# Laying out a convolution stage anew: more weight pairs in one product, low parts and tap sums on GpSimd, one-chunk first blocks, norm sums in two parts

## The chip, the core and the metric

The kernel runs on one core of a Trainium2 chip. The time is device microseconds of one execution, the median of several runs. A profile comes from one execution of its own, whose time is given beside it. In the rows, PE is TensorE's matmul side and PEld its weight load, DVE is VectorE, ACT is ScalarE, POOL is GpSimd (called Pool here) and SP is SyncE, whose queue issues the transfers. L226 is line 226 of the kernel's file.

## The reference

Two decoder layers are computed for a prompt of 256 positions and a group of 8 samples of one position each; the kernel treats them as T = 264 columns. The width is D = 2048, 16 chunks of 128 channels. Only the first mixer of the first layer is touched:

```python
def conformer_conv(x, past, w_in, b_in, w_dw, b_dw, ln_g, ln_b, w_out, b_out):
    a, gt = jnp.split(x @ w_in + b_in, 2, axis=-1)
    u = a * jax.nn.sigmoid(gt)
    y, new_past = causal_dwconv(u, past, w_dw, b_dw)      # 31 taps along the positions, per channel
    y = jax.nn.silu(layer_norm(y, ln_g, ln_b))
    return y @ w_out + b_out, new_past
```

Behind it come a ConvFFN, the per-layer embedding, an mLSTM mixer and a second ConvFFN, all with large weight products.

## The kernel before

Features lie on partitions, positions along the free axis. A weight product goes through `wblock`: it loads raw FP32 weights in buffers of four 128-row chunks (pool `rawp`, three buffers), and takes the chunks in pairs. A pair is normally split: ScalarE casts its high part (`whi`, L234), VectorE or Pool subtracts it from the raw weights to get the low part (`wlo`, L235), and TensorE forms three products per tile, `XH` by `whi`, `XL` by `whi` and `XH` by `wlo` (L250, L252, L253; L259 is the same product with `XL`, issued later). Where the argument `native` says so, the pair stays whole: one FP32 product of the raw weights with `X` (L226), which the trace records as two instructions. High and low parts have five buffers each (pool `hlp`), accumulators in PSUM six (`psA`), and U two (`psM`).

`conv_mixer` runs over `BLOCKS`, each of one or two chunks. A block forms for each chunk a gate and a value with `wblock` over all 16 input chunks (8 pairs). Then, per chunk:

- ScalarE takes the sigmoid of the gate (L546), VectorE writes U, the gated value, to PSUM (a `stt`), ScalarE copies it to SBUF (L555) and starts the sum: tap 30 with the bias into `Y` (L557), tap 29 into `Z`, a piece of `cscr` (L559).
- Taps 28 downward are shared out. The first `GT` of them: ScalarE scales (L564) into a ring in `cscr`, Pool adds into `Z`. The next `PT`: TensorE multiplies by diagonal matrices (L588), which Pool prepares at the start (L504), at the end of the stage (`late`). The rest: VectorE, one `stt` a tap from U into `Y`.
- `join` adds `Z` to `Y` on VectorE.

`SCM` says at which blocks the sample state is multiplied by its taps and reduced (four chunks at a time, on VectorE). `PLO` gives the number of low parts in 8 that Pool takes in each block, `NAT` the number of pairs left whole. In the last block `ln_pre` forms the layer norm's shift (a mean of chunks 0 to 11), subtracts it from those chunks and sums their squares; `ln` adds chunks 12 to 15, normalizes, and its results go into the first block of `cv_w_out`.

The order of each engine's instructions is made by a scheduler when the program is built, within the data's dependences; `high_priority` moves some ahead. Each engine then works through its queue in that order, so an instruction that waits holds everything behind it.

## Time and profile before

| | us |
|---|---|
| median of 3 runs (2585.0 to 2591.87) | 2591.32 |
| the profiled execution | 2594.45 |
| its span, first to last instruction | 2592.6 |
| TensorE busy, matmul | 2524.0 |
| VectorE busy | 1680.9 |
| ScalarE busy | 1286.0 |
| Pool busy | 395.2 |

The convolution stage fills the first tenth of the span: its weight products run from 4.3 us, and the first product with `cv_w_out` starts at 266.06 us. Over half of Pool's busy time lies in it. Records of matmuls overlap, so a busy TensorE is not one at its peak; the number of matmuls in a stretch tells more. Records of VectorE in a run overlap a little as well. A `stt` is shown as SCALAR_TENSOR_TENSOR at L141, an addition or subtraction by `tt` as TENSOR_TENSOR at L138, whichever engine runs it.

### The profile page before, as it was taken

The page shows a single profiled execution, that of the slowest core. Times are in us where ns is not written, and L with a number is a line of the kernel's source. Part 1 is how long each engine was busy: PE and PEld are TensorE (multiplying, and loading weights), DVE is VectorE, ACT ScalarE, POOL GpSimd, SP SyncE. Part 2 cuts the span into 40 slices and gives each one's busy share as a digit, 9 for nine tenths or more (in the row PEclk, how much of TensorE's full clock was granted, in tenths as well). Part 3 has the DMA queues.
Part 4 walks back from the last instruction along what each step waited for, and adds up shares of the span by engine and source line. Part 5 has one row for each costly group of instructions (what it writes and reads, how often), then busy time and mean ns, then how long its engine had stood idle before and what let it go on. Part 6 is the DMA issues. An engine that isn't in the chain of part 4 may idle for free.

```text
span 2592.6 us, 47730 instructions
## 1 busy us (share of the span) xinstructions
PE 2524.0 (97%) x20130; PEld 2499.7 (96%) x20130; DVE 1680.9 (65%) x2318; ACT 1286.0 (50%) x1801; POOL 395.2 (15%) x352
## 2 busy tenths in 40 slices
...
GB/s 251 172 132 203 164 149 194 177 187 182 182 180 179 179 179 207 180 167 195 208 225 217 238 242 214 220 148 196 188 181 179 179 179 179 180 180 204 178 175 138
DMA packets 266697, 486.57 MB, mean 188 GB/s; under 512 B 12362, under 2 KB 68426, under 8 KB 265938
## 3 DMA queue, kind: packets, MB, share of 16 engines
...
q14 instruction: 58, 0.48, 0.1%
...
## 4 chain that ended last, share of the span: by engine, by line
PE 83%; DVE 6%; DMA 3%; POOL 3%; issue 2%; ACT 2%; SPq 0%; POOLq 0%; DVEq 0%; ACTq 0%
PE acc L253 27%; PE acc L250 27%; PE acc L252 23%; PE acc L259 3%; DVE wlo L235 1%; POOL cscr L138 1%; DVE Y L141 1%; DMA X<-in_cT 1%; DMA out_cT<-X 1%; DVE spare L138 1%; DVE Y L138 1%; POOL wlo L235 1%; PE acc L452 1%; ACT whi L234 1%; POOL u L504 0%
## 5 line engine op out<-in xcount | busy, mean ns | idle before, releaser
L235 DVE TENSOR_TENSOR wlo<-raw,whi 128x1024 fp32r<-128x1024 f32 (+1 forms) x770 | 977.3, 1274 | 815.0 <-ACT whi L234 767.7
L234 ACT CAST whi<-raw 128x1024 fp32r<-128x1024 f32 x812 | 846.0, 1045 | 1019.9 <-PE acc L252 972.6
L253 PE MATMUL acc<-XH,wlo 128*128 128x264 f32 x4264 | 1192.0, 286 | 14.4 <-POOL wlo L235 7.9
L250 PE MATMUL acc<-XH,whi 128*128 128x264 f32 x4264 | 1193.7, 286 | 5.9 <-ACT cscr L546 4.9
L252 PE MATMUL acc<-XL,whi 128*128 128x264 f32 x3696 | 1049.7, 285 | 0.0
L253 PEld LDWEIGHTS acc<-XH,wlo 128*128 128x128 f32 x4264 | 803.7, 189 | 17.4 <-POOL wlo L235 9.6
L250 PEld LDWEIGHTS acc<-XH,whi 128*128 128x128 f32 x4264 | 801.7, 189 | 8.3 <-ACT cscr L546 5.3
L252 PEld LDWEIGHTS acc<-XL,whi 128*128 128x128 f32 x3696 | 701.4, 190 | 0.1
L235 POOL TENSOR_TENSOR wlo<-raw,whi 128x1024 fp32r<-128x1024 f32 (+1 forms) x42 | 97.4, 2324 | 1670.3 <-DVE X L138 1506.1
L253 PE MATMUL acc<-ha,wlo 128*128 128x264 f32 x1024 | 290.2, 285 | 0.0
L250 PE MATMUL acc<-ha,whi 128*128 128x264 f32 x1024 | 288.6, 285 | 0.0
L252 PE MATMUL acc<-ha,whi 128*128 128x264 f32 x960 | 272.0, 284 | 0.0
L250 PE MATMUL acc<-xo,whi 128*128 128x264 f32 x768 | 225.4, 295 | 8.0 <-ACT so L894 6.0
L253 PE MATMUL acc<-xo,wlo 128*128 128x264 f32 x768 | 223.8, 293 | 0.0
L252 PE MATMUL acc<-xo,whi 128*128 128x264 f32 x720 | 211.3, 294 | 0.0
L253 PEld LDWEIGHTS acc<-ha,wlo 128*128 128x128 f32 x1024 | 193.2, 189 | 0.0
L250 PEld LDWEIGHTS acc<-ha,whi 128*128 128x128 f32 x1024 | 192.0, 189 | 0.1
L252 PEld LDWEIGHTS acc<-ha,whi 128*128 128x128 f32 x960 | 181.4, 189 | 0.1
L250 PEld LDWEIGHTS acc<-xo,whi 128*128 128x128 f32 x768 | 148.9, 194 | 9.5 <-ACT so L894 6.4
L253 PEld LDWEIGHTS acc<-xo,wlo 128*128 128x128 f32 x768 | 149.1, 194 | 0.8
L252 PEld LDWEIGHTS acc<-xo,whi 128*128 128x128 f32 x720 | 139.6, 194 | 0.7
L138 POOL TENSOR_TENSOR cscr<-cscr 128x254 f32<-128x254 f32 (+10 forms) x140 | 124.7, 918 | 11.5 <-ACT cscr L564 10.3
(284 smaller groups left out, 2580.0 us busy)
## 6 DMA issues: line engine op xcount, KB each, us to landing
...
raw<-in_cv_w_in SPq DMA_DIRECT2D x48, 512.0 KB, 5.0
...
raw<-in_ml_w_in SPq DMA_DIRECT2D x32, 512.0 KB, 5.3
```

The source lines that it names most:

```text
L138: return e.tensor_tensor(o, a, b, op)
L141: return v.scalar_tensor_tensor(o, a, sc, b, op0, op1)
L234: whi = s.copy(hi[:, :, :width], r)
L235: wlo = e.tensor_tensor(lo[:, :, :width], r, f32(hi[:, :, :width]), ALU.subtract)
L250: pe.matmul(acc[j], wh, xh, start=kc == 0, stop=False)
L252: pe.matmul(acc[j], wh, xl, start=False, stop=False)
L253: wlast[0] = pe.matmul(acc[j], wl, xh, start=False, stop=not lag and kc == nk - 1)
L259: pe.matmul(acc[j], whs[j], xl, start=False, stop=lag > 0 and k0_ == nk - 1)
L452: po(pe.matmul(acc, w[:, k, j * P:(j + 1) * P], pt[:, k], start=k == 0, stop=k == 1))
```

## The change

- `BLOCKS` has ten blocks: chunks 0 and 1 come alone, then six pairs, then 14 and 15 alone as before.
- `NAT`: block 0 and the last block leave all 8 pairs whole, two-chunk blocks 3 of 8 (pairs 2, 5 and 7), block 1 three and block 8 four. Before, one pair was whole in each of blocks 0 and 1, three in the last but one, seven in the last.
- All low parts of the stage are on Pool (`loe=lambda k: g`); `PLO` is gone.
- `GT` is 6 in most blocks (9, 8 and 6 in the last three). ScalarE's scaled taps of both chunks go into one slot, and Pool adds them in one instruction of 2 x n elements. `join` likewise takes both chunks in one, runs one block later, and on Pool except for the last two blocks.
- `PT` is 2, 8 and 18 in the last three blocks: 30 diagonals in place of 37, and all their products in the last block.
- The sample state is multiplied on Pool, one group of four in each of blocks 1 to 4. Its bias and tap 30 are made by ScalarE, chunk by chunk, and added on Pool.
- The norm: `ln_first` at block 6 takes the shift from chunks 0 to 7, subtracts it and sums their squares; `ln_second` at block 8 adds chunks 8 to 11.

```diff
-BLOCKS = [(0, 2), (2, 2), (4, 2), (6, 2), (8, 2), (10, 2), (12, 2), (14, 1), (15, 1)]
-GT = [8, 7, 12, 6, 13, 8, 7, 11, 7]
-PT = {6: 4, 7: 9, 8: 20}
-NAT = [0, 1, 0, 0, 0, 0, 0, 3, 7]
-PLO = [0, 6, 8, 2, 3, 5, 5, 7, 4]
-SCM = {1: (0, 1), 2: (2, 3)}
+BLOCKS = [(0, 1), (1, 1), (2, 2), (4, 2), (6, 2), (8, 2), (10, 2), (12, 2), (14, 1), (15, 1)]
+GT = [6, 6, 6, 6, 6, 6, 6, 9, 8, 6]
+PT = {7: 2, 8: 8, 9: 18}
+NAT = [8, 3, 3, 3, 3, 3, 3, 3, 4, 8]
+PREPS = (6, 8)
+SCM = {1: (0,), 2: (1,), 3: (2,), 4: (3,)}
...
+    def ln_sum(Y, n):
+        a = t4("lna")
+        tt(a, Y[:, 0:4], Y[:, 4:8], ALU.add)
+        for q in range(2, n):
+            tt(a, a, Y[:, 4 * q:4 * q + 4], ALU.add)
         tt(a[:, 0:2], a[:, 0:2], a[:, 2:4], ALU.add)
         sd = t1("sd")
         tt(sd, a[:, 0], a[:, 1], ALU.add)
+        return sd
+
+    def ln_shift(Y, sd, n, pm):
         pe.matmul(pm[:, :T], onesD, sd, start=True, stop=True)
         c = t1("lnshift")
+        s.mul(c, pm[:, :T], float(D) / (4 * n * P))
+        stt(sd, c, -4.0 * n, sd, ALU.mult, ALU.add)
+        for q in range(n):
             tt(Y[:, 4 * q:4 * q + 4], Y[:, 4 * q:4 * q + 4], bc4(c), ALU.subtract)
+        return c
...
+    def ln_first(Y, sum2, pm):
+        sd = ln_sum(Y, 2)
+        c = ln_shift(Y, sd, 2, pm)
+        b = t4("lnb")
+        act(b, Y[:, 0:4], AF.Square)
+        b2 = t4("lnb2")
+        act(b2, Y[:, 4:8], AF.Square)
+        tt(b, b, b2, ALU.add)
+        tt(sum2[:, 0], b[:, 0], b[:, 1], ALU.add)
+        tt(sum2[:, 1], b[:, 2], b[:, 3], ALU.add)
+        return c, sd
+
+    def ln_second(Y, c, sd, sum2):
+        y = Y[:, 8:12]
+        tt(y, y, bc4(c), ALU.subtract)
+        b = t4("lnb")
+        act(b, y, AF.Square)
+        a = t4("lna")
+        tt(a[:, 0:2], Y[:, 8:10], Y[:, 10:12], ALU.add)
+        tt(b[:, 0:2], b[:, 0:2], b[:, 2:4], ALU.add)
+        tt(a[:, 0], a[:, 0], a[:, 1], ALU.add)
+        tt(sd, sd, a[:, 0], ALU.add)
+        tt(b[:, 0:2], b[:, 0:2], sum2, ALU.add)
...
+            wblock(W, [(D + c0 * P, n * P), (c0 * P, n * P)], x_rhs, NC, acc, loe=lambda k: g,
+                   native=lambda k, bi=bi: _pick(NAT[bi], k // 2), hook=load if bi == 0 else None, fine=bi == 0)
...
-                with tc.high_priority(PREP):
-                    shift, sd, sq = ln_pre(Y, accs(1)[0])
...
-                tt(xs, xs, w.unsqueeze(2).to_broadcast([P, 4, NB, 30]), ALU.mult)
+                tt(xs, xs, w.unsqueeze(2).to_broadcast([P, 4, NB, 30]), ALU.mult, e=g)
...
             for t in range(28, 28 - gt, -1):
+                z2 = slot(4, n)
                 for j in range(n):
-                    z2 = slot(4, 8)
-                    act(z2[:, 30 - t:SEQ], us4[:, (2 * bi + j) % 8, 0:226 + t], AF.Copy, scale=pc("cv_w_dw", (c0 + j) * CW + t))
-                    tt(Z[j][:, 30 - t:SEQ], Z[j][:, 30 - t:SEQ], z2[:, 30 - t:SEQ], ALU.add, e=g)
+                    act(z2[:, j, 30 - t:SEQ], U4[j][:, 0:226 + t], AF.Copy, scale=pc("cv_w_dw", (c0 + j) * CW + t))
+                tt(Z[:, :, 30 - t:SEQ], Z[:, :, 30 - t:SEQ], z2[:, :, 30 - t:SEQ], ALU.add, e=g)
+
+            def join(e, n=n, c0=c0, Z=Z):
+                o = Y[:, c0:c0 + n, 1:SEQ]
+                tt(o, o, Z[:, :, 1:SEQ], ALU.add, e=e)
+
+            while joins:
+                joins.pop(0)(g if bi < nb - 1 else v)
+            joins.append(join)
...
+            if bi == PREPS[0]:
+                sum2 = smp.tile([P, 2, T], F32, name="sum2", tag="sf")
+                shift, sd = ln_first(Y, sum2, accs(1)[0])
+            if bi == PREPS[1]:
+                sq = ln_second(Y, shift, sd, sum2)
```

The order of the instructions at three places follows. Names are those of the tiles; line numbers of the changed file are smaller by 3 in this part (L232 is the low part, L135 a `tt`, L138 a `stt`, L223 a whole product, L247 and L250 products with high and low part).

Pool after its setup, before: diagonals (`u`, `dg`), a piece of the ConvFFN's state (`sf`), then low parts and single adds of block 0's taps.

```order
L504 TENSOR_SCALAR u_110<-ident,par 128x128 x16
L504 TENSOR_SCALAR dg<-ident,par 128x128 x21
L138 TENSOR_TENSOR sf<-sf,par 128x44x8
L235 TENSOR_TENSOR wlo<-raw,whi 128x1024 x3
L138 TENSOR_TENSOR cscr<-cscr 128x254
L138 TENSOR_TENSOR cscr<-cscr 128x253
L235 TENSOR_TENSOR wlo<-raw,whi 128x1024
L138 TENSOR_TENSOR cscr<-cscr 128x252
L138 TENSOR_TENSOR cscr<-cscr 128x254
```

The same place now:

```order
L540 TENSOR_SCALAR u_110<-ident,par 128x128 x16
L540 TENSOR_SCALAR dg<-ident,par 128x128 x14
L232 TENSOR_TENSOR wlo<-raw,whi 128x2x256 x3
L135 TENSOR_TENSOR cscr<-cscr 128x254
L232 TENSOR_TENSOR wlo<-raw,whi 128x2x256
L135 TENSOR_TENSOR cscr<-cscr 128x253
L232 TENSOR_TENSOR wlo<-raw,whi 128x2x256
L135 TENSOR_TENSOR cscr<-cscr 128x252
```

There are seven diagonals fewer, `sf` is gone from here, and the low parts are those of block 1, half as wide. On TensorE, that block's first products (`acc_282`, `acc_283`) stand behind block 0's last whole ones:

```order
L223 MATMUL acc_112<-X,raw 128x264 x2
L223 MATMUL acc_113<-X,raw 128x264 x2
L247 MATMUL acc_282<-XH,whi 128x264
L247 MATMUL acc_283<-XH,whi 128x264
L250 MATMUL acc_282<-XH,wlo 128x264
L250 MATMUL acc_283<-XH,wlo 128x264
```

Before, block 0's split products followed its first whole pair, and their low parts came from VectorE.

Pool in the middle of the stage, before (around block 4): single adds of two chunks' taps, now and then a low part.

```order
L138 TENSOR_TENSOR cscr<-cscr 128x252
L138 TENSOR_TENSOR cscr<-cscr 128x254
L138 TENSOR_TENSOR cscr<-cscr 128x251
L138 TENSOR_TENSOR cscr<-cscr 128x253
L138 TENSOR_TENSOR cscr<-cscr 128x250
L235 TENSOR_TENSOR wlo<-raw,whi 128x1024
L138 TENSOR_TENSOR cscr<-cscr 128x252
L138 TENSOR_TENSOR cscr<-cscr 128x249
L138 TENSOR_TENSOR cscr<-cscr 128x251
L138 TENSOR_TENSOR cscr<-cscr 128x250
L235 TENSOR_TENSOR wlo<-raw,whi 128x1024
```

Pool in the middle of the stage now (taps of block 3, low parts of blocks 4 and 5, the join of block 3):

```order
L232 TENSOR_TENSOR wlo<-raw,whi 128x1024
L135 TENSOR_TENSOR cscr<-cscr 128x2x254
L135 TENSOR_TENSOR cscr<-cscr 128x2x253
L135 TENSOR_TENSOR cscr<-cscr 128x2x252
L135 TENSOR_TENSOR cscr<-cscr 128x2x251
L232 TENSOR_TENSOR wlo<-raw,whi 128x1024
L135 TENSOR_TENSOR cscr<-cscr 128x2x250
L232 TENSOR_TENSOR wlo<-raw,whi 128x1024
L135 TENSOR_TENSOR cscr<-cscr 128x2x249
L232 TENSOR_TENSOR wlo<-raw,whi 128x1024
L135 TENSOR_TENSOR Y<-Y,cscr 128x2x255
L232 TENSOR_TENSOR wlo<-raw,whi 128x1024
```

Adds cover two chunks each, every low part of the stage stands between them, and a join stands behind its block's adds.

VectorE from the last block's U (written to an accumulator) on, before: the norm's shift of chunks 0 to 11 comes next, three times 1056 wide.

```order
L141 SCALAR_TENSOR_TENSOR acc_2744<-acc_2655,par,cscr 128x256
L141 SCALAR_TENSOR_TENSOR us<-acc_2655,par,cscr 128x8
L141 SCALAR_TENSOR_TENSOR sd<-lnshift,sd 128x264
L138 TENSOR_TENSOR Y<-Y,lnshift 128x1056 x3
L138 TENSOR_TENSOR uw<-us,par 128x32
L235 TENSOR_TENSOR wlo<-raw,whi 128x1024
L138 TENSOR_TENSOR Y<-acc_2771,Y 128x247
L138 TENSOR_TENSOR Y<-Y,cscr 128x255
L138 TENSOR_TENSOR Y<-acc_2777,Y 128x247
L235 TENSOR_TENSOR wlo<-raw,whi 128x1024
L141 SCALAR_TENSOR_TENSOR Y<-acc_2744,par,Y 128x227
L138 TENSOR_TENSOR Y<-Y,uw 128x4x8
```

VectorE from the last block's U on, now: no shift of 1056 follows; taps of block 8, sums of the diagonals and a join stand there, with two low parts of `cv_w_out`.

```order
L138 SCALAR_TENSOR_TENSOR acc_2241<-acc_2190,par,cscr 128x256
L138 SCALAR_TENSOR_TENSOR us<-acc_2190,par,cscr 128x8
L138 SCALAR_TENSOR_TENSOR Y<-U,par,Y 128x228
L135 TENSOR_TENSOR Y<-acc_2273,Y 128x245
L138 SCALAR_TENSOR_TENSOR Y<-U,par,Y 128x227
L135 TENSOR_TENSOR Y<-acc_2277,Y 128x245
L138 SCALAR_TENSOR_TENSOR Y<-U,par,Y 128x226
L232 TENSOR_TENSOR wlo<-raw,whi 128x1024
L135 TENSOR_TENSOR Y<-Y,cscr 128x255
L232 TENSOR_TENSOR wlo<-raw,whi 128x1024
L135 TENSOR_TENSOR Y<-acc_2281,Y 128x246
L138 SCALAR_TENSOR_TENSOR Y<-acc_2241,par,Y 128x230
```

Behind the last embedding product of this norm (`acc` from `pw`) all five engines have the same instructions in the same order as before.

## Rows read from the trace of the kernel before

**Rows 1.** Busy time by stretch; columns named in the first line.
```profile
core 0: us, PE busy (x) PEld busy (x) DVE busy (x) ACT busy (x) POOL busy (x), PEclk, DMA share, GB/s
4.30:30.20 25.90, 25.90 (x184) 24.61 (x185) 15.66 (x24) 16.38 (x27) 15.67 (x26) 1.00 1.06 376
30.20:202.00 171.80, 154.93 (x1181) 151.40 (x1180) 160.93 (x299) 111.10 (x205) 162.49 (x141) 0.96 0.49 155
```

**Rows 2.** Who TensorE waited for, 0 to 230 us: total, times, longest.
```profile
PE acc L253 <- POOL wlo L235: 7.9, 7, 3.3
PE acc L253 <- DVE wlo L235: 6.5, 3, 2.8
PE acc L250 <- ACT cscr L546: 4.9, 2, 3.7
```

**Rows 3.** Busy time by stretch, columns as in rows 1: split products only.
```profile
280.00:300.00 20.00, 20.00 (x167) 20.00 (x166) 12.16 (x18) 8.39 (x10) 2.40 (x3) 1.00 0.48 159
```

**Rows 4.** Line 226: durations (min/median/max ns); then two runs: start, us, count.
```profile
L226 PE MATMUL acc<-X,raw x112: 383/386/777, 4.3 to 229.7; 128*128 128x264 f32 x112
...
204.75 1.94 PE L226 MATMUL acc<-X,raw 128*128 128x264 f32 x8
...
215.84 14.25 PE L226 MATMUL acc<-X,raw 128*128 128x264 f32 x56
```

**Rows 5.** Line 226 alone, by stretch: PE busy, PEld busy, PEclk, DMA share, GB/s.
```profile
215.80:218.00 2.20, 2.15 (x5) 1.73 (x6) 0.50 0.50 132
```

**Rows 6.** Groups by shape, 0 to 330 us: count, busy us, mean ns, idle before.
```profile
L234 ACT CAST whi<-raw 128x1024 fp32r<-128x1024 f32 x80 | 82.7, 1045 | 53.9 <-PE acc L252 21.8 <-DMA raw<-in_cv_w_in 20.7 <-PE acc L259 9.5
L235 DVE TENSOR_TENSOR wlo<-raw,whi 128x1024 fp32r<-128x1024 f32 x50 | 76.4, 1528 | 31.1 <-ACT whi L234 30.9
L235 POOL TENSOR_TENSOR wlo<-raw,whi 128x1024 fp32r<-128x1024 f32 x30 | 72.7, 2429 | 0.6 <-ACT whi L234 0.6
...
L138 POOL TENSOR_TENSOR cscr<-cscr 128x253 f32<-128x253 f32 x16 | 17.1, 1070 | 0.2
...
L235 POOL TENSOR_TENSOR wlo<-raw,whi 128x512 fp32r<-128x512 f32 x4 | 5.2, 1307 | 0.0
```

**Rows 7.** Pool in order of time, beside the taps of rows 8.
```profile
54.36 4.70 POOL L235 TENSOR_TENSOR wlo<-raw,whi 128x1024 fp32r<-128x1024 f32 x2
59.02 1.40 POOL L138 TENSOR_TENSOR cscr<-cscr 128x252 f32<-128x252 f32 x2
```

**Rows 8.** VectorE in order of time: a run of taps, then two joins.
```profile
56.72 8.64 DVE L141 SCALAR_TENSOR_TENSOR Y<-U,par,Y 128x243 f32<-128x243 f32 x23
...
204.91 2.75 DVE L138 TENSOR_TENSOR Y<-Y,cscr 128x255 f32<-128x255 f32 x1
...
219.06 0.41 DVE L138 TENSOR_TENSOR Y<-Y,cscr 128x255 f32<-128x255 f32 x1
```

**Rows 9.** Pool in order of time, the start: the diagonals.
```profile
14.53 11.42 POOL L504 TENSOR_SCALAR u<-ident,par 128x128 f32<-128x128 f32 x16 [12.44 <-DMA par<-in_par]
...
29.77 4.53 POOL L504 TENSOR_SCALAR dg<-ident,par 128x128 f32<-128x128 f32 x13
```

**Rows 10.** DMA issues, 40 to 180 us: KB each, median us to landing.
```profile
raw<-in_cv_w_in SPq DMA_DIRECT2D x40, 512.0 KB, 4.8
```

**Rows 11.** ScalarE in order of time, after the last weight product.
```profile
232.10 0.46 ACT L546 ACTIVATE cscr<-acc,par 128x264 f32<-128x264 f32 x1
236.89 0.37 ACT L555 COPY u<-acc 128x256 f32<-128x256 f32 x1 [1.76 <-DVE acc L141]
```

**Rows 12.** VectorE in order of time, the end of the stage.
```profile
237.24 6.28 DVE L138 TENSOR_TENSOR Y<-Y,lnshift 128x1056 f32<-128x1056 f32 x3
...
256.14 0.41 DVE L138 TENSOR_TENSOR Y<-acc,Y 128x247 f32<-128x247 f32 x1
```

**Rows 13.** TensorE in order of time: last diagonals, first product with cv_w_out.
```profile
238.72 8.58 PE L588 MATMUL acc<-u,dg 128*128 128x235 f32 x42
...
266.06 0.39 PE L250 MATMUL acc<-XH,whi 128*128 128x264 f32 x1 [0.23 <-ACT XH L368]
```

More of the change, by code (lines that the diff above doesn't have):

```diff
@@ L66 @@
 EC = 2
-N0 = (0,)
 LOE = (3, 7)
@@ L283, in ln_pre @@
         tt(sd, a[:, 0], a[:, 1], ALU.add)
[L284 removed]
+        return sd
+    def ln_shift(Y, sd, n, pm):
         pe.matmul(pm[:, :T], onesD, sd, start=True, stop=True)
         c = t1("lnshift")
[L287 to L289 removed]
+        s.mul(c, pm[:, :T], float(D) / (4 * n * P))
+        stt(sd, c, -4.0 * n, sd, ALU.mult, ALU.add)
+        for q in range(n):
             tt(Y[:, 4 * q:4 * q + 4], Y[:, 4 * q:4 * q + 4], bc4(c), ALU.subtract)
+        return c
+    def ln_pre(Y):
+        sd = ln_sum(Y, 3)
+        c = ln_shift(Y, sd, 3, misc("lnc"))
         b = t4("lnb")
@@ L488, in slot @@
             ring[0] += 1
-            return scr[:, first + ring[0] % n]
+            k = first + 2 * (ring[0] % 4)
+            return scr[:, k:k + n]
         us4, dg = hB(F32, "u4")
@@ L515, in conv_mixer @@
         blocks = BLOCKS
+        nb = len(blocks)
+        joins = []
         late = []
         for bi, (c0, n) in enumerate(blocks):
-            last = bi == len(blocks) - 1
+            last = bi == nb - 1
             acc = accs(2 * n)
-            wblock(W, [(D + c0 * P, n * P), (c0 * P, n * P)], x_rhs, NC, acc,
-                   loe=lambda k, bi=bi: g if _pick(PLO[bi], k // 2) else v,
-                   native=lambda k, bi=bi: _pick(NAT[bi], k // 2) or (bi == 0 and k // 2 in N0), hook=load if bi == 0 else None, fine=bi == 0)
+            wblock(W, [(D + c0 * P, n * P), (c0 * P, n * P)], x_rhs, NC, acc, loe=lambda k: g,
+                   native=lambda k, bi=bi: _pick(NAT[bi], k // 2), hook=load if bi == 0 else None, fine=bi == 0)
             if bi == DGB:
@@ L546, in conv_mixer @@
                 act(sg[:, j], acc[j], AF.Sigmoid, bias=pc("cv_b_in", NC + c0 + j))
-            Z = []
-            gt = GT[bi]
+            Z = scr[:, k0:k0 + n]
+            gt, pt = GT[bi], PT.get(bi, 0)
+            U4 = [us4[:, (2 * bi + j) % 8, :SEQ] for j in range(n)]
             for j in range(n):
                 ch, a = c0 + j, acc[n + j]
-                u = U[:, j, :SEQ]
+                u, w = U[:, j, :SEQ], U4[j]
                 stt(u, a[:, :SEQ], pc("cv_b_in", ch), sg[:, j, :SEQ], ALU.add, ALU.mult)
                 stt(us[:, ch], a[:, SEQ:], pc("cv_b_in", ch), sg[:, j, SEQ:], ALU.add, ALU.mult)
-                w = us4[:, (2 * bi + j) % 8, :SEQ]
                 s.copy(w, u)
```

53 lines of the change are left out of this document (18 added, 35 removed).

## The prediction

> **What bounds the kernel now.** The change ends before the first product with `cv_w_out`, and from the last embedding product on the instructions of all five engines stand in the same order before and after. So I forecast one number: the time W at which that first product starts. It is 266.06 us now [rows 13]; the 2326 us behind it I leave alone.
>
> I read the busy time by stretch first [rows 1]. From 30.2 to 202 us, six two-chunk blocks, Pool is busy 162.5 and VectorE 160.9 of 171.8 us, ScalarE only 111. TensorE looks busy too (154.9), but matmul records overlap, so I count work instead. Undisturbed split products come at 167 in 20.00 us, 0.120 us each [rows 3]; a weight tile costs three, 0.359. A block has 64 tiles, 23.0 us of work, and takes 171.8 / 6 = 28.6: over 5 us a block are lost. The waits of TensorE say to whom: low parts from Pool (7.9) and VectorE (6.5), accumulators that ScalarE has not read (4.9) [rows 2]. The rest goes in products at half clock or issued in dribs. Two helpers are full and TensorE is handed its low parts late.
>
> Why they are full: VectorE's low part has a mean of 1.53 us against Pool's 2.43 [rows 6], and VectorE's additions with two operands in SBUF are slowed whenever Pool works: the same 255-wide join took 2.75 us beside Pool's adds and 0.41 in a gap between them [rows 8]. Taps, which read U from PSUM, do not suffer: 23 in 8.64 us, 0.376 each, while Pool's low parts run at 4.70 for two [rows 7, 8].
>
> **The change part by part.** *Whole pairs on TensorE.* A whole product is two records. Eight of them are busy 1.94 us and one lasts 0.386, so they start every (1.94 - 0.386) / 7 = 0.222 us [rows 4]: 0.444 us a tile, 0.085 more than the split. The program has 56 such tiles now and 236 after. All weight tiles: now 456 x 0.359 + 56 x 0.444 = 188.6 us; after 276 x 0.359 + 236 x 0.444 = 203.9. On the bounding engine this part alone loses 15 us; it pays only by what it takes from the helpers.
>
> The Trainium skill's page "FP8 and Floating Point Precision", section "TensorE Precision Notes", says that a true FP32 product makes 4 passes through the array, which speaks against the change: four passes at the split's pace would be 0.48 us a tile and W some 7 us later. The trace has 0.444, and the sum goes by that.
>
> *The helpers.* VectorE gives up all its low parts here, 14 of 16 joins (one took 2.75, [rows 8]) and the sample multiplies; a two-chunk block leaves it 46 taps x 0.376 = 17.3 us and some 1.2 for U. Pool gets five low parts at about 2.35 (4.70 for two, [rows 7]), six merged adds and one merged join. No row has a merged add of 2 x 254. Its nearest row is the one-chunk low part, also two pieces of 256: 1.31 us [rows 6]; two single adds in a row take 1.40 [rows 7]; two slowed ones 2 x 1.07 = 2.14 (mean of the 253-wide, [rows 6]). I take 1.25, since Pool's back-to-back starts are a little closer than its durations and VectorE now hardly contends: 5 x 2.35 + 7 x 1.25 = 20.5 us a block, some 23 where a 960-wide sample multiply is added. ScalarE loses three casts a block. TensorE needs 24 x 0.444 + 40 x 0.359 = 25.0 us. So TensorE becomes the bound of the steady blocks, with 2 to 4 us of room on Pool.
>
> *A new wait.* Whole pairs read the raw weights directly, so their buffer comes free only when TensorE is past them. The buffer of pairs 4 and 5 of a block can be loaded once the block before has ended; pair 4 is due after three split pairs less one and a whole pair, 2 x 2.87 + 3.55 + 2.87 = 12.2 us into the block. The load takes 4.8 us [rows 10], the cast 1.05 [rows 6], the low part 2.35: 8.2. It fits with 4 us to spare, but while ScalarE waits for that load, its copies and taps queue behind the cast, and Pool stands at its low part. At each border the sigmoid must also free accumulators, and three casts stand ahead of it. I take 1 us for each of seven borders, 7 in all; bounds 0 and 20 (the 5 us lost per block now would give more, but those had two full helpers).
>
> *The start.* Block 0 is now whole: 32 x 0.444 = 14.2 us from 4.3, so it ends near 18.5 if the loads keep up. Block 1 needs a low part, and that comes from Pool alone, which first writes 30 diagonals (37 before). They wait for `par`: 14.53 now [rows 9]; half of the weight bytes in front of it are gone, so 13.5 (12 to 14.5). Beside VectorE's two-operand work 16 took 11.42 us, later 13 took 4.53 [rows 9]; 30 cost between 10.5 and 21.4. VectorE now has only the 16 splits of X there, so I stay near the low end: 14. With a low part of 1.3, block 1 starts at 13.5 + 14 + 1.3 = 28.8 (24 to 37). TensorE idles ten us there, and after an idle the clock falls: in block 8 it was granted 0.50 [rows 5], its upper to its lower level, and 56 records took 14.25 us where 0.222 each make 12.6 [rows 4]; I add 1.7.
>
> *End of the weight products*: 28.8 + 1.7 + (204 x 0.444 + 276 x 0.359 = 189.7) + 7 = 227.2, against 230.1 now.
>
> *The tail.* This is where most of the gain is. Now the sigmoid of the last chunk runs at 232.10, the copy of its u at 236.89 [rows 11], 42 diagonal records last until 247.3 [rows 13], and VectorE first does the norm's shift of twelve chunks, 6.28 us [rows 12], then its squares, and reaches the last sum at 256.14 [rows 12], 9.9 us ahead of W. After, the norm sums of chunks 0 to 11 are folded in at blocks 6 and 8, under the taps, where VectorE has six us a block to spare; without that cover the 6.28 us and the sums behind them would come back. What is late next is the chain of the last chunk itself. ScalarE: sigmoid, four residual scalings, two casts and the copy, which I put at 4.7 us after the end, a little under the 5.2 from that sigmoid to the end of its copy now [rows 11]; 36 records of its diagonals at 8.58 / 42 = 0.204 make 7.4, so 12; Pool's last six adds, behind its backlog and two pieces of the next stage's state, near 14 by the count of its queue at the prices above; then the same last 9.9 us. I take 24 (19 if the copy comes at once and Pool is done, 30 if Pool's backlog is a block deep).
>
> *Sum.* W = 227.2 + 24 = 251.2 against 266.06: 14.9 us gained. From the profiled execution's 2594.45 (span 2592.6 and 1.85 around it) that is 2579.6; that execution lies 3.1 above the median of the runs, 2591.32, and from the median I get **2576 us**.
>
> **The rivals.**
>
> *The helpers' slack is all real.* The diagonals go at their best (block 1 at 24), borders cost 1, the tail 22: W = 24 + 1.7 + 189.7 + 1 + 22 = 238.4, 28 gained, 2564 us. For it: VectorE has few two-operand additions left to disturb Pool. Against: three queues wait for each other at every border.
>
> *The bound doesn't move.* If load, cast and low part of pair 4 take over 12.2 us, as when ScalarE's cast waits behind taps that wait for Pool, each block keeps its 28.6 us. Six blocks then cost 6 x 3.6 = 21.6 in place of 7: W = 265.8, no change, 2591 us. For it: ScalarE and Pool do wait in line for raw weights after the change, and the present loss of 5 us a block has the same kind of hand-off. Against: the 4 us of room.
>
> *Slower: Pool is the new bound.* All low parts come from Pool. If merged adds cost two slowed single ones, 2.14 us, and low parts their mean of 2.43 [rows 6], a block needs 5 x 2.43 + 7 x 2.14 + 2.2 = 29.3 us of Pool against TensorE's 25.0. TensorE then waits 4.3 us in each of six blocks, mostly in one piece, and each such idle costs the 1.7 us at half clock again: 36 us in place of 7, W = 280, 2605 us. It turns slower from 22 us of border waits, some 3.6 a block. Against it: the 1.31 us row for the same shape [rows 6].
>
> The Trainium skill's "GPSIMD Engine Reference", section "4.1 Engine selection", puts elementwise work on VectorE, since GpSimd takes about twice as long on two inputs. The low parts agree in kind, and this rival is what the rule would do here; the sum of Pool's block says it fits all the same.
>
> *The change doesn't do what it says.* The order shows 14 of the 16 joins and every low part of the stage on Pool, and whole pairs at 2, 5 and 7 of each two-chunk block; I give it nothing.
>
> **How the numbers follow.** Forecast near 2576 (2568 to 2584): 0.58. Slack all real, 2564: 0.17. Bound doesn't move, 2591: 0.14. Pool the bound, 2605: 0.08. Some 0.03 for what I don't see. A measurement here can tell 0.3%, 7.8 us, so faster means below 2583.5. Faster: 0.17 and nearly all of 0.58, with a sliver of the rest, 0.77. Same: the third case and the forecast's upper edge, 0.15. Slower: 0.08. The range goes from 2560, below the best case's 2564 by what its start could still give, to 2589, between the forecast's bounds (all borders at 20, tail at 24 make 2589) and the unmoved case: it leaves out the slower case and about half of the unmoved one.
>
> **What would show it.** In the trace after: TensorE's wait for Pool's low part at the start, ending near 29; two-chunk blocks every 26 us with Pool idle part of each; merged adds of 1.25 to 1.35 us; joins gone from VectorE and its busy share well under 94% in the steady blocks; weight products ending near 227; W near 251; and 2326 us behind W as now. A merged add over 1.8 us, blocks of 28 us or more, or waits for raw weights on ScalarE of several us a block would make the prediction wrong on the slow side; a first low part near 24 and a tail of 20 on the fast side.

## The result, and the profile after

The changed kernel takes 2574.56 us (median of 4 runs, 2573.4 to 2577.84), the kernel before, beside it, 2591.6 (4 runs, 2585.0 to 2592.5): ratio 0.9939, 95% interval 0.9924 to 0.9954. The profiled execution after has a span of 2572.7 us, 19.9 less than before.

The first product with `cv_w_out` (W) starts at 254.33 us, where [rows 13] have 266.06 and the prediction 251.2. So 11.7 us of the 19.9 were won up to W and 8.2 behind it, where nothing was changed. Cut at the same sigmoids (29.86 and 199.32 before, 40.52 and 192.91 after) and at the end of the weight products (230.1 and 229.9), the 11.7 are a sum of gains and losses: the first two chunks take 10.7 us more, the six two-chunk blocks behind them 17.1 less, the last two chunks 6.2 more, and the tail from there to W 11.5 less (24.4 for 36.0). TensorE in order of time:

```profile
26.72 0.56 PE L250 MATMUL acc<-XH,wlo 128*128 128x264 f32 x1 [5.11 <-POOL wlo L232]
...
203.33 0.39 PE L247 MATMUL acc<-XH,whi 128*128 128x264 f32 x1 [2.64 <-ACT whi L231]
...
226.06 3.83 PE L223 MATMUL acc<-X,raw 128*128 128x264 f32 x16 [1.23 <-DMA raw<-in_cv_w_in]
...
254.33 0.39 PE L247 MATMUL acc<-XH,whi 128*128 128x264 f32 x1 [0.31 <-ACT XH L403]
```

The two-chunk blocks end when their sigmoids start on ScalarE: block 1 at 40.52, block 7 at 192.91. Busy time between the two (columns as in rows 1):

```profile
40.52:192.91 152.39, 151.67 (x1007) 141.91 (x1006) 111.27 (x269) 79.54 (x155) 129.50 (x82) 1.00 0.54 174
```

Six blocks in 152.39 us are 25.4 each. The prediction had 26, and 28.6 for before; from sigmoid to sigmoid the blocks before take 169.46 / 6 = 28.2, since the stretch of [rows 1] runs on to the last block's U. TensorE is busy throughout and at full clock; VectorE fell from 94% to 73% (111.27 of 152.39), Pool has 23 us of pauses. The waits of TensorE up to 230 us have changed their places (compare [rows 2]):

```profile
PE acc L250 <- POOL wlo L232: 6.6, 3, 5.1
PE acc L223 <- DMA raw<-in_cv_w_in: 5.3, 2, 4.1
PE acc L247 <- ACT whi L231: 2.6, 1, 2.6
```

The start: Pool's diagonals and block 1's first low parts. They end at 25.4 + 3.75 / 3 = 26.65; in [rows 9] the first 16 diagonals alone took 11.42.

```profile
13.61 6.97 POOL L540 TENSOR_SCALAR u<-ident,par 128x128 f32<-128x128 f32 x16 [11.52 <-DMA par<-in_par]
20.56 4.88 POOL L540 TENSOR_SCALAR dg<-ident,par 128x128 f32<-128x128 f32 x14
25.40 3.75 POOL L232 TENSOR_TENSOR wlo<-raw,whi 128x512 fp32r<-128x512 f32 x3
```

Pool's prices in the blocks 2 to 5 (67 to 170 us), as [rows 6] had them for the kernel before; the prediction took 2.35 and 1.25:

```profile
L232 POOL TENSOR_TENSOR wlo<-raw,whi 128x1024 fp32r<-128x1024 f32 x21 | 50.1, 2387 | 11.4 <-ACT whi L231 8.9 <-PE acc L250 2.3
L135 POOL TENSOR_TENSOR cscr<-cscr 128x508 f32<-128x508 f32 x4 | 5.1, 1284 | 0.0
```

The trouble comes after that, in blocks 8 and 9. By their tiles they need 32 x 0.444 + 16 x 0.444 + 16 x 0.359 = 27.1 us. They take 37.0, from 192.9 to 229.9. VectorE and Pool in order of time, ahead of them:

```profile
172.66 2.42 DVE L135 TENSOR_TENSOR Y<-Y,lnshift 128x1056 f32<-128x1056 f32 x2
...
179.28 3.95 DVE L135 TENSOR_TENSOR sum<-lnb 128x264 f32<-128x264 f32 x2
183.16 15.36 DVE L138 SCALAR_TENSOR_TENSOR Y<-U,par,Y 128x248 f32<-128x248 f32 x41
198.44 0.47 DVE L138 SCALAR_TENSOR_TENSOR U<-acc,par,cscr 128x256 f32<-128x256 f32 x1
...
201.15 1.26 POOL L135 TENSOR_TENSOR Y<-Y,cscr 128x510 f32<-128x510 f32 x1 [7.81 <-DVE Y L138]
203.35 1.48 POOL L232 TENSOR_TENSOR wlo<-raw,whi 128x512 fp32r<-128x512 f32 x1 [0.95 <-ACT whi L231]
```

VectorE is late from the first part of the norm sums on, so block 7's U comes at 198.44, five us after its sigmoid. Pool waits 7.81 us in the join of block 6 with block 8's low parts behind it, ScalarE's casts stand behind the copies of U, and TensorE stops. It then runs at the lower of its two clocks, as behind the idle at the start (columns as in rows 1):

```profile
26.90:30.20 3.30, 3.30 (x16) 3.30 (x17) 3.05 (x8) 2.50 (x7) 3.30 (x4) 0.50 0.30 87
204.40:211.00 6.60, 6.11 (x18) 5.18 (x19) 6.60 (x13) 5.39 (x12) 6.44 (x5) 0.50 0.58 182
```

The tail is as forecast: weight products end at 229.9, the copy of the last u is at 235.25, W comes 24.4 us after the end.

**Behind W.** Stretches from 1030 to 1370 us behind W, before and after (the mLSTM; columns as in rows 1):

```profile
1296.06:1636.06 340.00, 315.60 (x2444) 310.57 (x2443) 265.31 (x382) 204.54 (x415) 81.04 (x36) 0.96 0.69 231
1284.33:1624.33 340.00, 319.57 (x2512) 314.88 (x2511) 269.84 (x390) 208.68 (x419) 80.95 (x36) 0.97 0.70 234
```

The same instructions: 2512 matmuls after, 2444 before in the same time, at a granted clock of 0.97 and 0.96. Over all 14 profiles of this study (every kernel has the same work there) the time behind W lies between 2318.4 and 2326.6 us: seven with 0.97 in this stretch need 2318.4 to 2321.0, seven with 0.96 or 0.95 need 2322.8 to 2326.6. The four timed runs of `e2` differ by 9.7 us. Kernels near either end of the change lie on both sides: `e4`, the kernel before with one edit, has 2320.7, `e10`, the changed one with one edit, 2325.5. So these 8.2 us belong to the execution and not to the change. The timed runs share in it: the median less W is 2320.2 us for the changed kernel, the lowest of the 14 (the others 2321.9 to 2326.4, mean 2324.3). By that estimate 4 to 5 of the median's 17 us are chance. W is the better measure of the change, and the experiments are read by it.

### The profile page after: what moved, and what is told of

Its sections match the earlier page's. It is cut to its first block, busy times and chain, and to the rows that moved or that the text cites. A ratio compares the mean times of both kernels' runs of the same rounds, so it can differ in the third digit from the quotient of the medians.

```text
span 2572.7 us, 47195 instructions
## 1 busy us (share of the span) xinstructions
PE 2523.9 (98%) x19936; PEld 2490.0 (97%) x19936; DVE 1624.8 (63%) x2307; ACT 1254.9 (49%) x1762; POOL 361.9 (14%) x293
## 4 chain that ended last, share of the span: by engine, by line
PE 90%; DVE 4%; DMA 2%; ACT 2%; POOL 1%; issue 1%; SPq 0%; DVEq 0%; POOLq 0%; ACTq 0%
PE acc L250 28%; PE acc L247 28%; PE acc L249 25%; PE acc L256 3%; PE acc L223 2%; DVE wlo L232 1%; DVE spare L135 1%; PE acc L487 1%; DVE Y L138 1%; ACT whi L231 0%; DMA raw<-in_cv_w_in 0%; POOL wlo L232 0%; PE acc L263 0%; PE acc L262 0%; DMA raw<-in_cv_w_out 0%
## 5 line engine op out<-in xcount | busy, mean ns | idle before, releaser
L232 DVE TENSOR_TENSOR wlo<-raw,whi 128x1024 fp32r<-128x1024 f32 x742 | 926.5, 1254 | 804.3 <-ACT whi L231 758.7
L231 ACT CAST whi<-raw 128x1024 fp32r<-128x1024 f32 (+1 forms) x791 | 823.0, 1043 | 1058.3 <-PE acc L249 962.4
L247 PE MATMUL acc<-XH,whi 128*128 128x264 f32 x4084 | 1142.8, 286 | 3.2 <-ACT whi L231 2.6
L250 PE MATMUL acc<-XH,wlo 128*128 128x264 f32 x4084 | 1137.7, 285 | 6.6 <-POOL wlo L232 6.6
L249 PE MATMUL acc<-XL,whi 128*128 128x264 f32 x3516 | 996.1, 284 | 0.0
L250 PEld LDWEIGHTS acc<-XH,wlo 128*128 128x128 f32 x4084 | 767.3, 189 | 7.8 <-POOL wlo L232 7.3
L247 PEld LDWEIGHTS acc<-XH,whi 128*128 128x128 f32 x4084 | 764.9, 189 | 6.0 <-ACT whi L231 3.2
L249 PEld LDWEIGHTS acc<-XL,whi 128*128 128x128 f32 x3516 | 664.4, 189 | 0.6
L232 POOL TENSOR_TENSOR wlo<-raw,whi 128x1024 fp32r<-128x1024 f32 (+1 forms) x49 | 108.8, 2223 | 1691.7 <-DVE X L135 1506.1
L250 PE MATMUL acc<-ha,wlo 128*128 128x264 f32 x1024 | 290.0, 285 | 0.0
L247 PE MATMUL acc<-ha,whi 128*128 128x264 f32 x1024 | 288.4, 285 | 0.0
L247 PE MATMUL acc<-xo,whi 128*128 128x264 f32 x768 | 224.7, 294 | 8.3 <-ACT so L929 7.0
L250 PE MATMUL acc<-xo,wlo 128*128 128x264 f32 x768 | 222.4, 291 | 0.0
L250 PEld LDWEIGHTS acc<-ha,wlo 128*128 128x128 f32 x1024 | 193.1, 189 | 0.0
L247 PEld LDWEIGHTS acc<-ha,whi 128*128 128x128 f32 x1024 | 191.9, 188 | 0.1
L247 PEld LDWEIGHTS acc<-xo,whi 128*128 128x128 f32 x768 | 147.9, 193 | 9.9 <-ACT so L929 7.4
L250 PEld LDWEIGHTS acc<-xo,wlo 128*128 128x128 f32 x768 | 147.9, 193 | 0.7
L138 DVE SCALAR_TENSOR_TENSOR Y<-U,par,Y 128x229 f32<-128x229 f32 (+22 forms) x325 | 127.7, 455 | 28.5 <-ACT u L589 15.8
```

The lines of the kernel that those rows point to most:

```text
L138: return v.scalar_tensor_tensor(o, a, sc, b, op0, op1)
L231: whi = s.copy(hi[:, :, :width], r)
L232: wlo = e.tensor_tensor(lo[:, :, :width], r, f32(hi[:, :, :width]), ALU.subtract)
L247: pe.matmul(acc[j], wh, xh, start=kc == 0, stop=False)
L249: pe.matmul(acc[j], wh, xl, start=False, stop=False)
L250: wlast[0] = pe.matmul(acc[j], wl, xh, start=False, stop=not lag and kc == nk - 1)
```

## The experiments

All times in us. "End" is the end of the weight products of `cv_w_in`, W the first product with `cv_w_out`, both from one profile; the ratio is to the kernel before, from the timed runs. Where three kernels run the same instructions up to block 5 (the changed one, `e3`, `e8`), that block ends at 142.99, 143.20 and 142.59: differences of W under about 1 us mean nothing, and those of 2 or 3 us (`e3`, `e7`, `e8`) are weak, since each W is of one execution.

| | what | end | W | median | ratio (95%) |
|---|---|---|---|---|---|
| | before | 230.1 | 266.06 | 2591.6 | |
| | changed | 229.9 | 254.33 | 2574.56 | 0.9939 (0.9924 to 0.9954) |
| e1 | 2 of 8 whole | 228.9 | 255.64 | 2581.32 | 0.9955 (0.994 to 0.997) |
| e2 | block 1's low parts on VectorE | 222.6 | 245.79 | 2571.47 | 0.9927 (0.991 to 0.9944) |
| e3 | two joins on VectorE | 227.8 | 252.22 | 2577.78 | 0.9943 (0.9928 to 0.9958) |
| e4 | before, 3 of 8 whole | 229.2 | 259.03 | 2582.18 | 0.9969 (0.9956 to 0.9982) |
| e5 | none whole in two-chunk blocks | 253.0 | 275.13 | 2599.1 | 1.0029 (1.001 to 1.0047) |
| e6 | 3 of 5 low parts on VectorE | 237.3 | 262.27 | 2586.9 | 0.9979 (0.9968 to 0.9991) |
| e7 | single adds | 224.1 | 251.46 | 2575.73 | 0.9938 (0.9919 to 0.9957) |
| e8 | norm sums in one piece | 223.2 | 252.18 | 2574.51 | 0.9933 (0.9918 to 0.9948) |
| e9 | e2, fewer whole, more taps on Pool | 226.5 | 251.10 | 2573.24 | 0.9929 (0.9914 to 0.9944) |
| e10 | two-chunk first block | 226.3 | 250.76 | 2575.42 | 0.9944 (0.9928 to 0.996) |
| e11 | e2 + e7 + e8 + fewer whole | 227.1 | 254.50 | 2580.86 | 0.9967 (0.9956 to 0.9979) |
| e12 | e2 + e7 + e8 | 220.6 | 249.84 | 2571.74 | 0.9912 (0.9894 to 0.9931) |

**What pays: whole pairs, and low parts on one engine.** One part alone in the kernel before:

```diff
-NAT = [0, 1, 0, 0, 0, 0, 0, 3, 7]
+NAT = [0, 3, 3, 3, 3, 3, 3, 3, 7]
```

> The kernel before with one part of the change alone: 3 of 8 weight pairs whole in its blocks 1 to 7 (21 whole pairs instead of 4 there). Theory (helpers bound the blocks before, whole pairs take 3 casts and 3 low parts a block from them): TensorE's waits shrink and blocks go from 28.6 towards 26 us; the first product with cv_w_out comes near 256 to 260 instead of 266.06. Rival (contention of Pool and VectorE goes on to bound them, so whole pairs only make TensorE's own work 11 us longer): that product comes at 264 to 275.

W is 259.03: 7.0 of the 11.7 us come with this edit alone, though TensorE's own work grows by 17 pairs x 8 tiles x 0.085 = 11.6 us. W lies in the theory's range, but it didn't come there in the theory's way. Blocks still take 28.2 us (sigmoids from 30.07 to 199.00), so TensorE loses less in them but they get no shorter, and the weight products end only 0.9 us earlier. The other 6.1 us lie in the tail: VectorE, whose 1024-wide low parts up to 330 us take 64.8 us and not 76.4 [rows 6], makes the norm's shift 20 us earlier than in [rows 12]:

```profile
217.13 4.64 DVE L138 TENSOR_TENSOR Y<-Y,lnshift 128x1056 f32<-128x1056 f32 x3
```

The opposite, in the changed kernel:

```diff
-NAT = [8, 3, 3, 3, 3, 3, 3, 3, 4, 8]
+NAT = [8, 3, 0, 0, 0, 0, 0, 0, 4, 8]
```

> The changed kernel with no weight pair whole in its six two-chunk blocks (2 of 8 in an earlier run brought those ahead of the norm sums from 25.3 to 24.6 us). Theory (whole pairs are paid for on TensorE to keep Pool under it): Pool has 8 x 2.39 + 6 x 1.26 + 1.3 = 28 us of work a block against TensorE's 23.0, so blocks take 28 to 30 us; six of them 16 to 28 us more, the first product with cv_w_out at 268 to 282. Rival (Pool has more room than its busy time tells): blocks at 23 to 25 us, that product at 244 to 256.

W is 275.13 as expected, but it came there in another way: blocks 2 to 6 took 24 to 26 us, 24.7 on average (block 1's sigmoid at 41.82, block 6's at 165.16), no longer than with whole pairs, Pool doing their low parts first and putting off its adds. Then TensorE paid it all at once, ahead of block 7, at the ones product of the norm's shift, whose sums waited for those adds:

```profile
PE acc L286 <- DVE sd L135: 29.6, 1, 29.6
```

With the low parts of every second pair back on VectorE (three of a two-chunk block's five, as pairs 2, 5 and 7 are whole):

```diff
-acc, loe=lambda k: g,
+acc, loe=lambda k, bi=bi: v if 1 < bi < nb - 2 and k // 2 % 2 == 0 else g,
```

> The changed kernel with every second weight pair's low part on VectorE in the two-chunk blocks, as the kernel before divided them, so that VectorE and Pool both read two operands from SBUF. Theory (the change gains because VectorE keeps to the taps and Pool's adds run undisturbed): Pool's merged adds and low parts grow from 1.26 and 2.39 us, VectorE's low parts take 1.5 us and more, blocks grow from 25.3 towards 27 to 28 us and the first product with cv_w_out comes at 262 to 272 instead of 254.33. Rival (there is room on both, TensorE bounds either way): 253 to 257.

W is 262.27, 7.9 us later, in the theory's range, but its mechanism is not what the trace shows. Blocks 2 to 7 take 159.75 / 6 = 26.6 us. Low parts did get dearer, Pool's 2838 ns for the 2387 above and VectorE's 1583 for a mean of 1254 over the whole changed run. Of Pool's merged adds only the first of a block did (1666 for 1284); the five other shapes kept 1250 to 1291 ns, as in the changed kernel. Groups from 67 to 170 us:

```profile
L232 POOL TENSOR_TENSOR wlo<-raw,whi 128x1024 fp32r<-128x1024 f32 x8 | 22.7, 2838 | 24.2 <-ACT whi L231 24.2
L135 POOL TENSOR_TENSOR cscr<-cscr 128x508 f32<-128x508 f32 x4 | 6.7, 1666 | 9.0 <-ACT cscr L596 9.0
L135 POOL TENSOR_TENSOR cscr<-cscr 128x506 f32<-128x506 f32 x4 | 5.2, 1291 | 0.3
...
L232 DVE TENSOR_TENSOR wlo<-raw,whi 128x1024 fp32r<-128x1024 f32 x12 | 19.0, 1583 | 6.9 <-ACT whi L231 6.7
```

But from 40 to 200 us TensorE never waits for a low part. It waits for the sigmoids that free its accumulators, and ScalarE comes late to them because a cast stands ahead that waits for its raw weights:

```profile
PE acc L247 <- ACT cscr L580: 5.5, 4, 2.5
...
94.66 1.04 ACT L231 CAST whi<-raw 128x1024 fp32r<-128x1024 f32 x1 [11.32 <-DMA raw<-in_cv_w_in]
95.61 0.84 ACT L580 ACTIVATE cscr<-acc,par 128x264 f32<-128x264 f32 x2
```

These 5.5 us and the half clock from 97.6 to 101.0, behind the longest of these waits, some 1.7, make 7.2 of the 7.4 us that the six blocks grew. So `e6` shows what low parts on Pool alone are worth here; it doesn't show that contention is the reason.

**What doesn't pay: merged adds, one-chunk first blocks.**

```diff
-                tt(Z[:, :, 30 - t:SEQ], Z[:, :, 30 - t:SEQ], z2[:, :, 30 - t:SEQ], ALU.add, e=g)
+                    tt(Z[:, j, 30 - t:SEQ], Z[:, j, 30 - t:SEQ], z2[:, j, 30 - t:SEQ], ALU.add, e=g)
```

> The changed kernel with each merged tap sum made as two adds of one chunk, as before. Theory (an undisturbed single add is 0.69 us from start to start in block 1 of the changed kernel, so two are 1.4 against 1.25 merged: 6 x 0.15 = 0.9 us more a block on Pool, which is idle for 4): no change, the first product with cv_w_out at 253.5 to 256. Rival (single adds cost the 1.07 us that they took before): 6 x 0.9 = 5.3 us a block, Pool becomes the bound at 26 to 27 us a block, that product at 260 to 266.

A single add is 0.72 to 0.79 us without contention. Pool has 7.7 us more to do in six blocks (137.16 against 129.50) and they take as long (152.06). W is even 2.9 earlier, below the range expected: blocks 8 and 9 lose less. Which order of instructions does that was not taken apart, and the medians (2575.73 and 2574.56) don't show it.

```diff
-BLOCKS = [(0, 1), (1, 1), (2, 2), (4, 2), (6, 2), (8, 2), (10, 2), (12, 2), (14, 1), (15, 1)]
+BLOCKS = [(0, 2), (2, 2), (4, 2), (6, 2), (8, 2), (10, 2), (12, 2), (14, 1), (15, 1)]
```

> The changed kernel with its two one-chunk blocks at the start replaced by one two-chunk block, all of it whole, as the kernel before began; everything else of the change stays. Theory (Pool's 30 diagonals, done at 25.4 us, are what the one-chunk start runs into): the first block lasts about 28 us on TensorE, to 34 to 37, so the low parts of the next one are there when it ends and the 5.1 us wait is gone; whole instead of split tiles cost 20 x 0.085 = 1.7 us; VectorE gets its first U some 12 us later. The first product with cv_w_out comes at 247 to 252. Rival (the one-chunk start earns time, because VectorE and ScalarE get their first taps 12 us earlier and else run late for the rest): 256 to 264.

W is 250.76, 3.6 us better than with one-chunk blocks, as the theory had it: the 5.1 us wait is gone, and the last two blocks still take 36.8. The medians (2575.42 and 2574.56) don't show it.

**The start.**

```diff
-acc, loe=lambda k: g,
+acc, loe=lambda k, bi=bi: v if bi == 1 else g,
```

> The changed kernel with the five low parts of the second block (its first one with split weights) on VectorE instead of Pool. Theory (TensorE's wait of 5.1 us before that block is for Pool, which writes 30 diagonals first, until 25.40 us): the first low part is there about 2 us after its cast, near 21, the wait shrinks from 5.1 to under 1 us, and less half clock follows (up to 1.7 us); the first product with cv_w_out comes at 248 to 250 instead of 254.33. Rival (the block is held by its casts or its transfer, or the gain is given back at the next wait for Pool): 253 to 255.

W is 245.79, 8.5 us earlier and better than expected. VectorE makes the first two low parts at 20.73 and TensorE goes on at 21.61 instead of 26.72:

```profile
20.73 1.42 DVE L232 TENSOR_TENSOR wlo<-raw,whi 128x512 fp32r<-128x512 f32 x2 [1.69 <-ACT whi L231]
```

Only 2.9 us of it are there when block 1 ends (sigmoid at 37.67 instead of 40.52), since TensorE then waits 1.7 us for the block's later casts and low parts, and the lower clock comes all the same (granted 0.50 from 30.7 to 33.9); 4.0 when block 7 ends. Another 3.3 come in blocks 8 and 9, which take 33.7 instead of 37.0, and 1.3 in the tail.

**The stall ahead of block 8.**

```diff
-joins.pop(0)(g if bi < nb - 1 else v)
+joins.pop(0)(g if bi < nb - 3 else v)
```

> The changed kernel with the last two joins that Pool makes (of blocks 6 and 7) on VectorE. Theory A (the stall of TensorE near 201 to 212 us comes from Pool, which waits 7.8 us in that join for VectorE's taps with the low parts of block 8 queued behind it): the stall goes, with it the half clock near 205 to 212 (3.4 us), and the first product with cv_w_out comes at 248 to 250. Theory B (the stall comes from VectorE being late itself, by the first part of the norm sums, and reaches TensorE through ScalarE too, whose casts stand behind the copies of U): TensorE still waits about 2.6 us for the cast, and that product comes at 252 to 255.

W is 252.22: theory B. Pool no longer waits for the join; it waits for the cast instead, which stands behind the copies of U:

```profile
202.78 1.28 POOL L232 TENSOR_TENSOR wlo<-raw,whi 128x512 fp32r<-128x512 f32 x1 [9.28 <-ACT whi L231]
```

The half clock near 205 to 212 did go, but that and the join together are worth 2.1 us. So it is VectorE that is late, and that by the norm sums:

```diff
-PREPS = (6, 8)
+PREPS = (-1, -1)
...
+                shift, sd, sq = ln_pre(Y, accs(1)[0])
```

> The changed kernel with the norm sums made in one piece in the last block, as before. Theory of the prediction (their two parts lie beside other work, and the tail behind the weight products is 24.4 instead of 36.0 us for it): the tail grows by 6 to 11 us, the first product with cv_w_out at 258 to 264. Rival (the first part is what made VectorE late before block 8 and stalled TensorE near 201 to 212 us): the weight products end 5 to 7 us earlier, at 223 to 225 instead of 229.9, the tail grows all the same, and that product comes at 251 to 258.

The rival of the prediction's theory held: weight products end 6.7 us earlier (223.2), the tail grows by 4.6 (29.0), W is 2.1 earlier. By W, folding the norm sums in cost more than it brought; the medians are alike.

**Where the norm sums' time goes.** Two edits were meant to take TensorE's surplus back:

```diff
-NAT = [8, 3, 3, 3, 3, 3, 3, 3, 4, 8]
+NAT = [8, 3, 2, 2, 2, 2, 2, 2, 4, 8]
```

> The changed kernel with 2 instead of 3 of 8 weight pairs whole in its six two-chunk blocks. Theory (TensorE bounds these blocks): 6 blocks x 8 tiles x (0.444 - 0.359) = 4.1 us less on TensorE; Pool, which was idle for about 4 us of a 25.3 us block in the trace of the changed kernel, takes the sixth low part of 2.4 us. The first product with cv_w_out (254.33 us in the changed kernel) comes at 250 to 251, the run is 3 to 4 us shorter. Rival (the helpers bind as soon as one low part is added, by Pool or by the chain cast, low part, product): blocks grow to 26 us or more and that product comes at 255 to 260.

Theory and rival were half right each. Blocks 2 to 5 came down to 24.6 us (sigmoids from 39.33 to 137.69), 6.4 us gained by the U of block 5. Block 6 then took 32.9 and gave all of it back. VectorE, then TensorE, in block 6:

```profile
162.77 6.74 DVE L135 TENSOR_TENSOR Y<-Y,lnshift 128x1056 f32<-128x1056 f32 x2
...
171.05 0.59 PE L247 MATMUL acc<-XH,whi 128*128 128x264 f32 x1 [4.73 <-ACT cscr L580]
```

The subtraction of the shift, two times 1.21 us in the changed kernel, took two times 3.4; the squares on ScalarE waited for it, and the sigmoids that free TensorE's accumulators stood behind the squares. Edits of `e9`: `e2`, NAT 2 in blocks 2 to 4, GT 8 in blocks 5 and 6.

> The changed kernel with three moves together: block 1's low parts on VectorE (alone, it brought the first product with cv_w_out from 254.33 to 245.79), 2 instead of 3 of 8 weight pairs whole in blocks 2 to 4 (alone and in six blocks, it brought the end of block 5 from 145.05 to 138.65 and gave it back in block 6, where the norm sums stand), and two more taps of blocks 5 and 6 through ScalarE and Pool instead of VectorE (2 x 2 x 2 x 0.38 = 3.0 us less on VectorE). Theory: 3 x 0.68 = 2.0 us from whole pairs and 1 to 3 us from the earlier taps, that product at 241 to 244. Rival (VectorE's lateness at block 6 is set by the norm sums' slow adds, not by taps; what is gained ahead of it is given back there): 245 to 247.

W is 251.10, later than with `e2` alone: worse than either expectation. With more work on Pool the norm's adds were slow again (a 1056-wide one 3.42 us) and block 7's U came 7 us after its sigmoid, so that TensorE waited 5.7 for a cast that stood behind U's copies. `e11` puts `e2`, `e7`, `e8` and NAT 2 in blocks 2 to 6 together:

> The changed kernel with four moves that were each tried alone: block 1's low parts on VectorE (product with cv_w_out 8.5 us earlier), norm sums in one piece in the last block (2.1 us), single tap adds on Pool (2.9 us), and 2 instead of 3 of 8 pairs whole in blocks 2 to 6 (6 us by block 5, given back at the norm sums). Theory A (they add up, since the norm sums' slow adds were what gave gains back): weight products end near 210, the tail is 28 to 30, the product with cv_w_out comes at 238 to 241 and the run takes 2561 to 2567 us. Theory B (the first three remove one and the same stall ahead of block 8, so only the first and the last add up): 242 to 246 and 2566 to 2572 us.

W is 254.50, outside both ranges. VectorE and Pool in order of time:

```profile
150.14 14.88 DVE L135 TENSOR_TENSOR lna<-Y 128x1056 f32<-128x1056 f32 x1
...
151.07 2.40 POOL L232 TENSOR_TENSOR wlo<-raw,whi 128x1024 fp32r<-128x1024 f32 x1
153.43 1.40 POOL L135 TENSOR_TENSOR cscr<-cscr 128x252 f32<-128x252 f32 x2
154.79 4.73 POOL L232 TENSOR_TENSOR wlo<-raw,whi 128x1024 fp32r<-128x1024 f32 x2
159.46 1.41 POOL L135 TENSOR_TENSOR cscr<-cscr 128x251 f32<-128x251 f32 x2
160.81 2.41 POOL L232 TENSOR_TENSOR wlo<-raw,whi 128x1024 fp32r<-128x1024 f32 x1
163.16 0.74 POOL L135 TENSOR_TENSOR cscr<-cscr 128x250 f32<-128x250 f32 x1
174.04 0.72 POOL L135 TENSOR_TENSOR cscr<-cscr 128x254 f32<-128x254 f32 x1 [10.14 <-ACT cscr L597]
```

One add that takes 1.26 us elsewhere lasts 14.88, and ends one us after Pool's queue ran empty at 163.9. Pool had no pause in between, its instructions no slower than usual. The last run puts the whole pairs back, with `NAT` as in the change:

> The run of four moves, with 3 of 8 weight pairs whole in blocks 2 to 6 again (TensorE 5 x 0.68 = 3.4 us more, Pool and ScalarE one pair a block less). In the run of four moves, VectorE's 128x1056 add of the norm sums lasted 14.88 us, from 150.14 until Pool's queue ran empty at 164, and block 6 began 6 us late. Theory (an add of two SBUF operands on VectorE gets through only in Pool's pauses, so the whole pairs pay by the pauses they leave): the same add takes under 3 us, no wait of 5 us before block 6, and the first product with cv_w_out comes at 243 to 249 instead of 254.50, though TensorE has more to do. Rival (the slow add was a chance of that run, and TensorE's work decides): 255 to 259.

VectorE's add, then Pool beside it:

```profile
145.21 1.77 DVE L135 TENSOR_TENSOR lna<-Y 128x1056 f32<-128x1056 f32 x1 [1.82 <-POOL Y L135]
...
143.88 1.30 POOL L135 TENSOR_TENSOR Y<-Y,cscr 128x510 f32<-128x510 f32 x1
145.14 0.73 POOL L135 TENSOR_TENSOR cscr<-cscr 128x254 f32<-128x254 f32 x1
145.83 3.38 POOL L232 TENSOR_TENSOR wlo<-raw,whi 128x1024 fp32r<-128x1024 f32 x1
149.17 0.73 POOL L135 TENSOR_TENSOR cscr<-cscr 128x253 f32<-128x253 f32 x1
```

The add takes 1.77 us, block 6 follows without a wait, and W is 249.84, 4.7 us earlier with more work on TensorE (0.8 above the expected range). But the theory's reason fails: Pool has no pause there either. The add lets the one instruction end that Pool is in, then runs, and Pool's next low part takes 3.38 instead of 2.40: the two engines take turns. The slow adds of `e1` and `e9` look the same, 3.42 us beside a low part that ends and a next one that is stretched to 3.4. Why the add of `e11` was passed over by ten more of Pool's instructions is open, and that it was a chance of that run is not excluded. The scheduler moved that add within VectorE's queue too, so `e12` is not the one edit alone. With 2571.74 us, `e12` and `e2` (2571.47) are the two fastest; their intervals overlap that of the change.

## Why the prediction was right, and where it was not

The time was forecast as 2576 and is 2574.56, but errors cancel in it, and that it came so near is luck. From the profiled execution's time the forecast took 14.9 us for W and 3.1 for the median; the trace took 11.7 for W (254.33 for 251.2) and 8.2 behind it. With the mean of the other kernels behind W, 2324.3, the same W would give 2578.6 (an estimate), still near the forecast.

- *Whole pairs, the helpers.* The sum was right: in the steady blocks TensorE waits 0.7 us in all and takes 25.4 for 25.0 of work a block, and Pool's prices are 2.39 and 1.28 for 2.35 and 1.25. `e4`, `e5` and `e6` show that whole pairs and low parts on Pool are worth their microseconds, but not by the path forecast. Whole pairs don't make the blocks shorter: with them alone blocks keep 28.2 us and the tail gains (`e4`), without them blocks take 24.7 and the norm sums pay, waiting for Pool's adds (`e5`). Of the 2.8 us a block that were won, `e6` gives back 1.2; merged adds are worth nothing (`e7`). The rest came with the other parts, of which fewer taps, the joins and the sample multiplies on Pool were not tried alone.
- *The new wait for raw weights.* It is there (ScalarE's casts waited 14.0 us for transfers and 18.4 for whole products from 67 to 170 us) and is hidden. Two-chunk blocks lose 0.4 us each where the prediction gave every border 1. In `e6` it is not hidden: the hand-off that the prediction described, casts ahead of the sigmoids that free accumulators, costs TensorE 5.5 us there.
- *The start.* Block 0's whole products ended near 21.4 and not 18.5, so TensorE idled 5.1 us and not ten. Block 1's first low product came at 26.72 for 28.8, since 30 diagonals took 11.85 us and not 14; the half clock behind the idle is in the records for 3.4 us, half of which, 1.7, is lost, as forecast. The sum took the wait itself as given; `e2` shows that it could be avoided.
- *The end of the weight products*: 229.9 for 227.2. Ahead of block 8 the sum was 6 us better than forecast: with block 1's tiles at 12 x 0.444 + 20 x 0.359 = 12.5, 26.72 + 1.7 + 12.5 + 6 x 25.4 = 193.3 (measured 192.9), where the prediction's numbers give 28.8 + 1.7 + 12.5 + 6 x 26 = 199. Blocks 8 and 9 then lost 9.9 us, for which 1 or 2 stood in the sum.
- *The step that failed*: that the norm sums could be "folded in at blocks 6 and 8, under the taps, where VectorE has six us a block to spare". Spare time is not what they need. They add two operands from SBUF, which the prediction itself had read as slowed beside Pool [rows 8], and it did not carry that over to them. Nor did the room suffice: in block 6 they took VectorE 8.6 us (0.94 + 2.42 + 1.26 + 3.95) and 1.8 of waiting for ScalarE's squares; the last two sums, 3.95 here, take 0.76 in `e1`, where Pool pauses. Having the sums there cost 6.7 us of weight products and won 4.6 of tail (`e8`).
- *The tail* was right (24.4 for 24), and with 11.5 us it is "where most of the gain is". But the prediction put it down to the norm sums, which give 4.6; 6.1 come with whole pairs alone (`e4`), which the prediction counted for the blocks.
- *The rivals.* None happened. Pool as the bound is near in `e5`, where it reaches TensorE through the norm sums and not in the steady blocks. The Trainium skill's "GPSIMD Engine Reference", section "4.1 Engine selection", would have put low parts on VectorE; `e6` did that with three of five and lost 7.9 us.
- *The range*, 2560 to 2589, held.
